# Two-layer hybrid decoder trunk: mixer with projections by halves, an earlier values product, regrouped output pairs, and modulation rows issued two ahead

## The chip, the cores and the metric

The kernel runs on one core of one Trainium2 chip. The metric is the device time of one execution in microseconds (us); the median of the runs is compared. The core's engines are TensorE (PE, matmuls; PEld for its weight loads), VectorE (DVE), ScalarE (ACT), GpSimd (POOL) and SyncE (SP), whose queue issues nearly all the DMAs here.

## The reference

Two layers over a sequence of 256 tokens of width 1024, in float32. Each layer is a half-step SwiGLU FFN, a token mixer and a second half-step FFN. Every sublayer has an RMS norm with a shift, a scale and a gate (nine modulation vectors of 1024 per layer), which come from a conditioning vector by a product with `w_ada`.

```
mod = split(silu(c) @ w_ada[l] + b_ada[l], 9)
h = rms_norm(x, ffn1_norm) * (1 + mod[1]) + mod[0]
x = x + 0.5 * (1 + mod[2]) * swiglu(h, ffn1_w_gu, ffn1_w_down)
h = rms_norm(x, mix_norm) * (1 + mod[4]) + mod[3]
x = x + (1 + mod[5]) * hybrid_mixer(h, ...)
h = rms_norm(x, ffn2_norm) * (1 + mod[7]) + mod[6]
x = x + 0.5 * (1 + mod[8]) * swiglu(h, ffn2_w_gu, ffn2_w_down)
```

The mixer projects h to a query latent (384), a key/value latent (256), a rotary key (32) and three convolution parts (512 each). The latents are normalised and expanded to 8 heads, followed by causal attention. The convolution group is a gate times a causal convolution of three taps. Both groups are normalised, concatenated and projected back to 1024. One RMS norm ends the trunk.

## The kernel before, in words

**Data.** Channels lie on the 128 partitions, tokens on the free axis: `x` is 8 tiles of 128 x 256. A float32 product is made of reduced-precision float32 matmuls: a factor is split into a high part (ScalarE, a copy into `fp32r`) and a low part (VectorE, the difference), and `mm3` sums high x high, high x low and low x high, three matmuls of 256 columns per 128 x 128 tile of weights. `mm3w` does the same with one matmul of 512 columns and one of 256.

**The weight stream.** All weights are a stream of chunks of 16 tiles (128 x 2048, 1 MB), numbered in the order of use: 22 gate/up and 11 down chunks for an FFN, 17 for a mixer. `load` (L235) takes the next one: a DMA on SP into `raw`, then high pieces on ScalarE (L262) and low pieces on VectorE (L265), two pieces for a chunk in the FFNs, four for most in the mixer. `raw`, `hi` and `lo` have three buffers each. Chunks 0 to 32 are layer 0's first FFN, 33 to 49 its mixer.

**The modulation rows.** The products with `w_ada` are 144 row tiles of 128 x 1024 (0.5 MB), each read by a DMA on SP (`ada_load`, L180) into one of four buffers and reduced by one VectorE instruction (L189) to a column of `mods`. `PACE` says how many rows must be done by which chunk (`ada_target`): in the down projection of layer 0's first FFN about two a chunk and more, in the mixers 6 over 16 chunks, in layer 0's second FFN and layer 1's first about one a chunk. In `load`, the chunk's DMA comes first and then its rows: DMA and product.

**Who sets the order.** SP runs its instructions in program order everywhere. TensorE does so in the mixer. A planner at compile time orders the others: it walks through a modelled time and gives each engine, among the instructions that are ready, the one that is due first. `due` sets the due time relative to a clock of matmul work; the `SLACK` table, `SPLIT_LEAD` and `ADA_SLACK` are such offsets. An instruction due late is still run early if its engine has nothing else ready. The order on each engine is then fixed, and the chip follows it, waiting where something is late.

**The mixer.** `ORDER` (L42) is the order of its steps, a letter each:
- `K`, `Q`, `P`: the projections to the key/value latent, the query latent, and its last third with the rotary key; four steps of 12 matmuls each make the two outputs of a chunk (`proj`, L604). `c` and `d` are the convolution's input and its gates, four chunks' and two chunks' worth of steps.
- `X`: the sum over channels for the mixer's RMS norm (a float32 matmul with a tile of ones, `Stat.rstd`). `L`, `Z`: the same for the latents. `N`, `V`, `v`: keys and values.
- `q0` to `q3`, `s0` to `s3`, `t0` to `t3`, `a0` to `a3`: queries, scores and softmax, transposes, and the product with the values of a head pair. `av_part` (L736) also copies the product out and adds its square to the attention's statistic.
- `n`, `m`: the sum and the norm of the attention output and of the convolution output.
- `A`, `B`: the output projection's steps over the two halves (`out`, L779). After every second `B` step a pair of output channels tiles is whole: residual (L394), then `put` for each tile, which makes the next FFN's input `u` in two parts (L351, L357) and adds the tile's square to the next norm's statistic (L318, L322).
- `w`: loads the next chunk ahead of its use. After `m`, a guard makes all later splits and modulation products follow the last instructions of m's norm.

`residual` and `put` also end the down projection of an FFN, so that the mixer's first step stands behind them.

Of the kernel before, what the change touches and what calls it, by code (L numbers as in the profile page):

```python
# [18 lines left out]
P = 128  # L19
L = 2  # L20
D = 1024
S = 256
KD = D // P
FF = 2816
NJ = FF // P
# [6 lines left out]
CH = 16 * P  # L32
WHOLE = 4
ADA_SLACK = 10000
ROPE_SLACK = 20000
LATE = 4
PACE = (0, 0), (8, 16), (21, 32), (33, 58), (49, 64), (84, 97), (117, 130), (133, 136), (146, 144)
# [1 line left out]
ENGS = {'p': mybir.EngineType.PE, 's': mybir.EngineType.SP, 'v': mybir.EngineType.DVE, 'a': mybir.EngineType.Activation}  # L39
MAN = 'sp'  # L40
SM_ACT = 2
ORDER = ("K K K X K Q Q P Q Q P P L c c c P c N Z V v q0 q1 s0 q2 c c c c t0 s1 a0 q3 c c c t1 c a1 s2 s3 c c c c t2 d d a2 t3 d d a3 "  # L42
         "d n w d w d d A A A w m A A w A A A B B B B B B B B").split()
WIN = dict(K=0, Q=1, P=2, c=3, d=7)
WO = dict(A=0, B=2)
SLACK = {'B': 6000, 'K': -2000, 'L': -4000, 'N': 0, 'P': 6000, 'Q': 0, 'V': 1000, 'X': 6000, 'Z': -4000, 'a': -4000, 'c': 6000, 'd': 0, 'm': 6000, 'n': 0, 'q': 2000, 's': -6000, 't': -4000}
CUTS = 4
GUARD = ('m',)
MIX_SPLIT, MIX_ADA = 2000, 2000
# [5 lines left out]
ADA_ORDER = [(0, m * 8 + i) for i in range(8) for m in (1, 0)]  # L55
# [64 lines left out]
def trunk(ctx: ExitStack, tc, x_d, c_d, pos_d, small_d, cst_d, ada_d, gu1_d, dn1_d, win_d, up_d, wo_d, gu2_d, dn2_d, out_d):  # L120
# [25 lines left out]
    x = one.tile([P, KD, S], F32, name="x")  # L146
# [4 lines left out]
    uL, uH = u[:, :, 0:S], u[:, :, S:]  # L151
# [59 lines left out]
    for l in range(L):  # L211
# [4 lines left out]
        n = {}  # L216
# [18 lines left out]
    def load(apart=False, head=False):  # L235


        i = taken[0]
        taken[0] += 1
        src, n, cuts = stream[i][:3]  # L240
        z0 = stream[i][3] if len(stream[i]) > 3 else 0
        raw = wp.tile([P, CH], F32, tag="raw", name=nm("raw"), bufs=3)
        hi = wp.tile([P, CH], F32R, tag="hi", name=nm("hi"), bufs=3)
        lo = wp.tile([P, CH], F32R, tag="lo", name=nm("lo"), bufs=3)
        if head:
            ada_load(1)
            nc.sync.dma_start(raw[:, :z0], src[:, :z0])
            ada_load(2)
            nc.sync.dma_start(raw[:, z0:n], src[:, z0:n])
        else:  # L250
            due(-LOAD_LEAD)
            nc.sync.dma_start(raw[:, :n], src)
            due(lead[1])
            with ExitStack() as es:
                for q in guard:
                    es.enter_context(tc.issue_after(q))
                ada(ada_target(i + 1))
        c = (n - z0) // cuts
        zs = [slice(z0 + q * c, z0 + (q + 1) * c) for q in range(cuts)]

        def top(q):
            nc.scalar.activation(hi[:, zs[q]], raw[:, zs[q]], AF.Copy)  # L262

        def rest(q):
            nc.vector.tensor_tensor(lo[:, zs[q]], raw[:, zs[q]], f32(hi[:, zs[q]]), ALU.subtract)  # L265

        if apart:
            return (raw, hi, lo), top, rest
        with ExitStack() as es:
            for q in guard:  # L270
                es.enter_context(tc.issue_after(q))
            for q in range(cuts):
                due(c / 128 * 322 * q - lead[0])
                top(q)
                rest(q)
        return raw, hi, lo
# [4 lines left out]
    def due(t):  # L281

        tc.cur_priority = int(clock[0] + t)
# [6 lines left out]
    def mm3(dst, w, t, aH, aL, first, last, ext=0):  # L290
        hi, lo = w[-2:]
        n = S + ext
        wh = hi[:, t * P:(t + 1) * P]
        wl = lo[:, t * P:(t + 1) * P]
        mm(dst[:, :n], wh, aH[:, :n], start=first, stop=False, skip_group_check=True)
        mm(dst[:, :S], wh, aL, start=False, stop=False, skip_group_check=True)
        mm(dst[:, :n], wl, aH[:, :n], start=False, stop=last, skip_group_check=True)
# [61 lines left out]
    class Pre:  # L359
# [20 lines left out]
            nc.scalar.activation(hcol, sh, AF.Copy)  # L380
            nc.vector.tensor_tensor(lcol, sh, f32(hcol), ALU.subtract)

        def put(self, k):
            g = self.scale(k)
            hi_of(uH[:, k, :S], x[:, k, :], g)
            lo_of(uL[:, k, :], uH[:, k, :S], x[:, k, :], g)
            self.stat.add(x[:, k, :])


    def residual(src, m, l, sub, f, halves=False):  # L390
# [177 lines left out]
    def mixer(l, pre, nxt):  # L568
        mf = one.tile([P, NJ, S], F32, tag="aH", name=nm("mf"))
        mr = one.tile([P, NJ, S], F32R, tag="aL", name=nm("mr"))  # L570
        ckv, cq, conv, V, K = mf[:, 0:2], mf[:, 2:5], mf[:, 5:9], mf[:, 9:13], mf[:, 13:21]
# [32 lines left out]
        def proj(t, evac):  # L604

            n = seen[t] = seen.get(t, -1) + 1
            if n % 4 == 0:
                open_[t] = chunk(), ps_tile()
            w, pt = open_[t]
            i = n % 4 // 2  # L610
            for k in range(n % 2 * 4, n % 2 * 4 + 4):
                mm3(pt[:, i, :], w, i * KD + k, uH[:, k, :], uL[:, k, :], k == 0, k == KD - 1, 2)
            if n % 4 == 3:
                due(SLACK[t])
                evac(scaled(pt))
# [163 lines left out]
        def out(t):  # L779
            n = seen[t] = seen.get(t, -1) + 1  # L780
            half = "AB".index(t)
            zH, zL = ((atH, atL), (cvH, cvL))[half]
            g, i = divmod(n, 4)
            if not acc:
                acc.extend((ps_tile(), ps_tile()))
            if i == 0:
                open_[t] = chunk()
            w = open_[t]
            steps = [(m, i) for m in range(4)] if half == 0 else [(m, k) for k in range(i % 2 * 2, i % 2 * 2 + 2) for m in
                                                                  (i // 2 * 2, i // 2 * 2 + 1)]  # L790
            for m, k in steps:
                m += 4 * g
                dst = acc[m // 2 % 2][:, g, (m % 2) * S:(m % 2 + 1) * S]
                mm3(dst, w, m % 4 * 4 + k, zH[:, k, :], zL[:, k, :], half == 0 and k == 0 and m % 2 == 0, half == 1 and k == 3)
            if half == 1 and i % 2 == 1:
                due(SLACK["B"])
                for q in (i - 1, i):
                    m = 4 * g + q
                    residual(acc[m // 2 % 2][:, g, (m % 2) * S:(m % 2 + 1) * S], m, l, 1, 1.0)
                    nxt.put(m)  # L800
                    if m == 5:
                        nxt.shifts()

        do = dict(K=lambda: proj("K", kv_evac), Q=lambda: proj("Q", q_evac), P=lambda: proj("P", qk_evac),
                  c=lambda: proj("c", conv_evac), d=lambda: proj("d", gate_evac), X=lambda: pre.stat.rstd(r, t=SLACK["X"]), L=kv_norm, N=keys, Z=q_norm,
                  V=lambda: values(0), v=lambda: values(1), n=lambda: head_norm("n", sat, attn, O_AN, atH, atL),
                  m=lambda: head_norm("m", scv, conv, O_CN, cvH, cvL), A=lambda: out("A"), B=lambda: out("B"))
# [96 lines left out]
def _layout(a):  # L904
    g = {}
# [17 lines left out]
    for f in (1, 2):  # L923
        t = _tiles(a[f"ffn{f}_w_gu"]).reshape(L, KD, 2, NJ, P, P)
        w = t.transpose(0, 3, 4, 1, 2, 5).reshape(L, NJ, P, CH)
        if f == 1:
            head = w[0, :8].reshape(8, P, 8, 2, P).transpose(2, 1, 0, 3, 4).reshape(1, 8, P, CH)
            w = np.concatenate([np.concatenate([head, w[:1, 8:]], axis=1), w[1:]], axis=0)
        g[f"gu{f}"] = np.ascontiguousarray(w)
        t = _tiles(a[f"ffn{f}_w_down"]).transpose(0, 2, 1, 3, 4).reshape(L, 11, 16, P, P)  # L930
# [6 lines left out]
    for i, s in [(i, s) for i in range(4) for s in (1, 2)] + [(i, 0) for i in range(4)]:  # L937
        parts.append(w[:, :, o + s * CW + i * P:o + s * CW + (i + 1) * P])
    t = _tiles(np.concatenate(parts, axis=2))
    t = t.transpose(0, 2, 1, 3, 4).reshape(L, 9, 16, P, P)  # L940
    g["win"] = np.ascontiguousarray(t.transpose(0, 1, 3, 2, 4).reshape(L, 9, P, CH))
    uk = a["w_ukv"].reshape(L, 2, P, H, 128)
    nope = uk[..., :64].reshape(L, 2, P, 4, P).transpose(0, 2, 3, 1, 4).reshape(L, P, 1024)
# [30 lines left out]
```

## Time and profile before

| what | value |
| --- | --- |
| median of 3 runs | 999.11 us (997.51 to 999.49) |
| the profiled execution | 1002.27 us |
| its span, first to last instruction | 1000.5 us |
| mean granted clock of TensorE | 0.994 |
| DMA moved | 250.78 MB, mean 251 GB/s |

All rows are of the profiled execution. A timeline row gives the start in us from the start of the span, the duration, the engine, the line of the kernel, the operation, out<-in by the program's names, the form, the count of instructions merged, and in brackets the engine's idle time before it with what ended it. SPq is SP's queue of DMAs: its rows are the issues, and a wait of the queue shows as a late issue. A row of waits gives total us, times, and the longest.

### The profile page before, as it was taken

Reading aid. Unit: us, or ns where it says so; the run is one execution under the profiler, and the core shown is the slowest. Engines: PE = TensorE matmul, PEld = TensorE weight load, DVE = VectorE, ACT = ScalarE, POOL = GpSimd, SP = SyncE. Lnnn points to the kernel's source line nnn. Section 1 sums busy time; section 2 is a strip of 40 time slices with the busy share of each in tenths; the row PEclk is TensorE's granted clock in tenths of the full one; section 3 lists DMA queues with packets and bytes.
Section 4 is the critical chain, followed back from the end, with each engine's and each line's share of the span. In section 5 each row is a group of like instructions: output and inputs, shape, how many; then the busy total and the mean of one; then the engine's idle time right before and its main releaser. Section 6 shows DMA issues by size and latency. Waiting matters only on the chain.

```text
span 1000.5 us, 16812 instructions
## 1 busy us (share of the span) xinstructions
PE 977.1 (98%) x6560; PEld 898.1 (90%) x6560; DVE 854.1 (85%) x1598; ACT 581.3 (58%) x1010; POOL 8.0 (1%) x27
## 2 busy tenths in 40 slices
PE   9999999999999999999999999998999999999996
PEld 7999998899989988888998888888998998888885
DVE  5899999999999998988899878877799999766653
ACT  4465544467856755654486555543687676656541
POOL 0000110000000000000000000000000000000000
PEclk9999999999999999999999999998999999999998
DMA  9999998874746687877768777776355547655531
GB/s 348 376 361 340 336 320 324 311 282 154 275 178 253 234 318 253 301 267 291 270 219 324 279 258 283 277 255 214 124 217 193 200 171 290 215 178 201 173 122 43
DMA packets 47007, 250.78 MB, mean 251 GB/s; under 512 B 5504, under 2 KB 5824, under 8 KB 26576
## 3 DMA queue, kind: packets, MB, share of 16 engines
q1 hardware_dynamic: 46224, 248.81, 68.3%
q8 instruction: 51, 0.84, 0.3%
q10 hardware_dynamic: 288, 0.65, 0.2%
q0 software_dynamic: 416, 0.25, 0.1%
q14 instruction: 28, 0.23, 0.1%
HBM read 248.59 MB, written 1.10 MB: 250 GB/s over the span
## 4 chain that ended last, share of the span: by engine, by line
PE 78%; DVE 11%; DMA 7%; issue 1%; ACT 1%; SPq 0%; DVEq 0%; ACTq 0%
PE ps L287 78%; DMA ada<-in_ada 6%; DVE lo L265 5%; DVE ada L189 1%; DVE x L394 1%; DMA raw<-in_gu 1%; DVE acc L322 1%; DVE u L357 1%; PE ps L731 1%; DVE mr L355 1%; ACT hi L262 0%; DMA cb<-in_c 0%; DVE nt L594 0%; ACT mr L351 0%; DVE mf L767 0%
## 5 line engine op out<-in xcount | busy, mean ns | idle before, releaser
L287 PE MATMUL ps<-u,hi 128*128 128x256 f32 (+2 forms) x2464 | 599.8, 324 | 6.5 <-ACT u L351 3.7
L287 PE MATMUL ps<-u,lo 128*128 128x256 f32 (+1 forms) x1664 | 470.1, 283 | 1.1 <-DVE lo L265 1.1
L287 PEld LDWEIGHTS ps<-u,hi 128*128 128x128 f32 x2464 | 413.5, 190 | 46.4 <-ACT u L351 4.3
L265 DVE TENSOR_TENSOR lo<-raw,hi 128x1024 fp32r<-128x1024 f32 (+2 forms) x384 | 394.8, 1046 | 41.4 <-ACT hi L262 40.9
L262 ACT ACTIVATE hi<-raw 128x1024 fp32r<-128x1024 f32 (+2 forms) x384 | 338.3, 912 | 113.4 <-PE ps L287 48.9
L287 PEld LDWEIGHTS ps<-u,lo 128*128 128x128 f32 x1664 | 315.9, 190 | 1.4 <-DVE lo L265 1.4
L287 PE MATMUL ps<-a,hi 128*128 128x512 f32 (+1 forms) x792 | 248.6, 372 | 1.4 <-DVE a L355 1.4
L189 DVE CUSTOM_DVE_ANT_0 ada<-ada,cb,small 128x1024 f32<-128x1024 f32 x144 | 183.1, 1280 | 33.4 <-DMA ada<-in_ada 32.8
L287 PE MATMUL ps<-a,lo 128*128 128x256 f32 x704 | 197.9, 281 | 0.0
L287 PEld LDWEIGHTS ps<-a,hi 128*128 128x128 f32 x792 | 143.0, 189 | 29.8 <-DVE a L355 1.7
L287 PEld LDWEIGHTS ps<-a,lo 128*128 128x128 f32 x704 | 133.2, 189 | 0.0
L351 ACT ACTIVATE a<-cc 128x256 fp32r<-128x256 f32 x88 | 36.3, 415 | 68.0 <-DVE cc L413 56.3
L287 PE MATMUL ps<-mr,hi 128*128 128x256 f32 x384 | 70.6, 285 | 0.0
L351 ACT ACTIVATE u<-x,gs 128x256 fp32r<-128x256 f32 x40 | 20.3, 507 | 84.6 <-DVE x L394 84.6
L287 PEld LDWEIGHTS ps<-mr,hi 128*128 128x128 f32 x384 | 60.2, 192 | 0.8 <-issue 0.3
L287 PE MATMUL ps<-mr,lo 128*128 128x256 f32 x192 | 54.3, 283 | 0.0
L394 DVE SCALAR_TENSOR_TENSOR x<-ps,gate,x 128x256 f32<-128x256 f32 x76 | 35.9, 480 | 19.2 <-PE ps L287 18.5
L355 DVE TENSOR_TENSOR a<-cc,a 128x256 fp32r<-128x256 f32 x88 | 37.0, 422 | 16.0 <-ACT a L351 15.8
L412 ACT ACTIVATE cc<-g 128x256 f32<-128x256 f32 x54 | 22.5, 418 | 41.5 <-DVE g L411 41.5
L411 DVE TENSOR_TENSOR g<-ps,g 128x512 f32<-128x512 f32 x54 | 37.0, 685 | 0.7 <-ACT g L410 0.6
L287 PEld LDWEIGHTS ps<-mr,lo 128*128 128x128 f32 x192 | 36.8, 191 | 0.0
L410 ACT ACTIVATE g<-ps 128x512 f32<-128x512 f32 x54 | 31.2, 578 | 0.0
(121 smaller groups left out, 568.4 us busy)
## 6 DMA issues: line engine op xcount, KB each, us to landing
raw<-in_gu SPq DMA_DIRECT2D x87, 1024.0 KB, 5.8
ada<-in_ada SPq DMA_DIRECT2D x144, 512.0 KB, 6.2
raw<-in_dn SPq DMA_DIRECT2D x44, 1024.0 KB, 5.2
raw<-in_win SPq DMA_DIRECT2D x18, 1024.0 KB, 5.7
raw<-in_wo SPq DMA_DIRECT2D x8, 1024.0 KB, 4.8
raw<-in_up SPq DMA_DIRECT2D x2, 1024.0 KB, 5.9
raw<-in_up SPq DMA_DIRECT2D x2, 768.0 KB, 4.4
raw<-in_up SPq DMA_DIRECT2D x4, 384.0 KB, 3.1
```

The lines of the kernel that those rows point to most:

```text
L189: nc.vector.tensor_tensor_reduce(out=a, in0=a, in1=cb, scale=1.0, scalar=sm(l, t), op0=ALU.mult, op1=ALU.add, accum_out=mods[l][:, t:t + 1])
L262: nc.scalar.activation(hi[:, zs[q]], raw[:, zs[q]], AF.Copy)
L265: nc.vector.tensor_tensor(lo[:, zs[q]], raw[:, zs[q]], f32(hi[:, zs[q]]), ALU.subtract)
L287: nc.tensor.matmul(dst, a, b, **kw)
L322: nc.vector.tensor_tensor(self.acc, self.acc, t, ALU.add)
L351: nc.scalar.activation(dH, src, AF.Copy, scale=scale)
L355: nc.vector.tensor_tensor(dL, src, f32(dH), ALU.subtract)
L357: nc.vector.scalar_tensor_tensor(dL, src, scale, f32(dH), ALU.mult, ALU.subtract)
L394: nc.vector.scalar_tensor_tensor(x[:, m, :], s, g, x[:, m, :], ALU.mult, ALU.add)
L410: nc.scalar.activation(t2, pg[:, :, :S], AF.Copy)
L411: nc.vector.tensor_tensor(t2, pg[:, :, S:], t2, ALU.add)
L412: nc.scalar.activation(sg, t2[:, 0, :], AF.Silu)
```

## The change

Five edits:
1. `proj` runs its four steps as two halves of the input channels: steps 0 and 1 take channels 0-3 of the first and the second output, steps 2 and 3 take channels 4-7. The host lays the tiles of the projection chunks out in that order. At the mixer's start `K K K X K Q Q P Q Q P P` becomes `K K Q Q K X K Q Q P P P`.
2. `t3 d d a3 d n` becomes `t3 d a3 d d n`: a3 one `d` step earlier, n where it was.
3. One `w` less, the others later: the chunks of A are asked for one by one, the first of B after `m`, the second at its use.
4. After a pair of output tiles, both residuals come first, then both `put` without the square, and then both squares with a due time of their own (`y`). The pair's due time falls from 6000 to 1500 ns, and to 0 for the last pair.
5. From chunk 33 on (`AHEAD_FROM`), `load` issues the rows' DMAs before the chunk's, and up to two rows beyond the target. The products stay with their chunk.

```
+ADA_AHEAD, AHEAD_FROM = 2, NJ + 11
...
-ORDER = ("K K K X K Q Q P Q Q P P L c c c P c N Z V v q0 q1 s0 q2 c c c c t0 s1 a0 q3 c c c t1 c a1 s2 s3 c c c c t2 d d a2 t3 d d a3 "
-         "d n w d w d d A A A w m A A w A A A B B B B B B B B").split()
+ORDER = ("K K Q Q K X K Q Q P P P L c c c P c N Z V v q0 q1 s0 q2 c c c c t0 s1 a0 q3 c c c t1 c a1 s2 s3 c c c c t2 d d a2 t3 d a3 "
+         "d d n d w d d A A A w m A A w A A A B B B B B B B B").split()
...
-SLACK = {'B': 6000, 'K': -2000, ...
+SLACK = {'B': 1500, 'y': 5000, 'K': -2000, ...
...
             due(-LOAD_LEAD)
+            if i >= AHEAD_FROM:
+                ada_load(min(ada_target(i + 1) + ADA_AHEAD, len(ADA_ORDER)))
             nc.sync.dma_start(raw[:, :n], src)
...
-        def put(self, k):
+        def put(self, k, add=True):
...
-            self.stat.add(x[:, k, :])
+            if add:
+                self.stat.add(x[:, k, :])
...
-            i = n % 4 // 2
-            for k in range(n % 2 * 4, n % 2 * 4 + 4):
-                mm3(pt[:, i, :], w, i * KD + k, uH[:, k, :], uL[:, k, :], k == 0, k == KD - 1, 2)
+            i, h = n % 2, n % 4 // 2
+            for k in range(4 * h, 4 * h + 4):
+                mm3(pt[:, i, :], w, 4 * (n % 4) + k % 4, uH[:, k, :], uL[:, k, :], k == 0, k == KD - 1, 2)
...
-                due(SLACK["B"])
-                for q in (i - 1, i):
-                    m = 4 * g + q
+                pair = 4 * g + i - 1, 4 * g + i
+                due(SLACK["B"] if n < 7 else 0)
+                for m in pair:
                     residual(acc[m // 2 % 2][:, g, (m % 2) * S:(m % 2 + 1) * S], m, l, 1, 1.0)
-                    nxt.put(m)
-                    if m == 5:
-                        nxt.shifts()
+                for m in pair:
+                    nxt.put(m, False)
+                if n == 5:
+                    nxt.shifts()
+                due(SLACK["y"])
+                for m in pair:
+                    nxt.stat.add(x[:, m, :])
...
-    t = t.transpose(0, 2, 1, 3, 4).reshape(L, 9, 16, P, P)
+    t = t.transpose(0, 2, 1, 3, 4).reshape(L, 9, 2, 2, 4, P, P).swapaxes(2, 3).reshape(L, 9, 16, P, P)
```

More of the change, by code (lines that the diff above doesn't have):

```diff
@@ L41 @@
 SM_ACT = 2
-ORDER = ("K K K X K Q Q P Q Q P P L c c c P c N Z V v q0 q1 s0 q2 c c c c t0 s1 a0 q3 c c c t1 c a1 s2 s3 c c c c t2 d d a2 t3 d d a3 "
-         "d n w d w d d A A A w m A A w A A A B B B B B B B B").split()
+ORDER = ("K K Q Q K X K Q Q P P P L c c c P c N Z V v q0 q1 s0 q2 c c c c t0 s1 a0 q3 c c c t1 c a1 s2 s3 c c c c t2 d d a2 t3 d a3 "
+         "d d n d w d d A A A w m A A w A A A B B B B B B B B").split()
 WIN = dict(K=0, Q=1, P=2, c=3, d=7)
 WO = dict(A=0, B=2)
-SLACK = {'B': 6000, 'K': -2000, 'L': -4000, 'N': 0, 'P': 6000, 'Q': 0, 'V': 1000, 'X': 6000, 'Z': -4000, 'a': -4000, 'c': 6000, 'd': 0, 'm': 6000, 'n': 0, 'q': 2000, 's': -6000, 't': -4000}
+SLACK = {'B': 1500, 'y': 5000, 'K': -2000, 'L': -4000, 'N': 0, 'P': 6000, 'Q': 0, 'V': 1000, 'X': 6000, 'Z': -4000, 'a': -4000, 'c': 6000, 'd': 0, 'm': 6000, 'n': 0, 'q': 2000, 's': -6000, 't': -4000}
 CUTS = 4
```

## The prediction

> **What bounds the kernel now.** I read the page first, then TensorE's busy time in stretches of 10 us, then its own rows wherever a stretch was not full, and from each of those back to what released it.
>
> ```profile
> PE 977.1 (98%) x6560; PEld 898.1 (90%) x6560; DVE 854.1 (85%) x1598; ACT 581.3 (58%) x1010; POOL 8.0 (1%) x27
> ```
>
> TensorE (PE) is busy for 977.1 of 1000.5 us. In a full stretch it starts a 256-column matmul every 0.12 us, and nothing in the change takes a matmul away. So the change can only move TensorE's waits. These are the waits next to the code it touches, from TensorE's timeline (start, duration, then the idle time before it and what ended it):
>
> ```profile
> 206.99 0.39 PE L287 MATMUL ps<-u,lo 128*128 128x258 f32 x1 [1.14 <-DVE lo L265]
> ...
> 283.29 0.67 PE L287 MATMUL ps<-acc,ones 128*128 128x256 f32 x2 [1.47 <-DVE acc L322]
> ...
> 317.15 0.38 PE L287 MATMUL ps<-u,hi 128*128 128x258 f32 x1 [0.41 <-ACT u L351]
> ...
> 318.53 0.38 PE L287 MATMUL ps<-u,hi 128*128 128x256 f32 x1 [1.00 <-DVE u L357]
> ...
> 694.73 0.39 PE L287 MATMUL ps<-u,hi 128*128 128x258 f32 x1 [2.59 <-ACT u L351]
> ...
> 695.78 0.58 PE L287 MATMUL ps<-u,hi 128*128 128x256 f32 x1 [0.67 <-DVE u L357]
> ...
> 772.41 0.67 PE L287 MATMUL ps<-acc,ones 128*128 128x256 f32 x2 [1.47 <-DVE acc L322]
> ...
> 806.44 0.38 PE L287 MATMUL ps<-u,hi 128*128 128x258 f32 x1 [0.69 <-ACT u L351]
> 807.82 0.38 PE L287 MATMUL ps<-u,hi 128*128 128x256 f32 x1 [1.00 <-DVE u L357]
> ```
>
> Each layer has three places: the mixer's first projection (206.99; 694.73 and 695.78), the sum "n" over the attention output (283.29; 772.41), and the way out into the second FFN (317.15 and 318.53; 806.44 and 807.82). Together the waits are 10.4 us. The wait at 694.73 costs more than itself, as stretches of TensorE show (us, busy time and count of each engine, then granted clock, DMA share, GB/s):
>
> ```profile
> 210.00:220.00 10.00, 10.00 (x85) 9.95 (x84) 9.42 (x19) 6.55 (x15) 0.00 (x0) 1.00 0.92 333
> 695.05:701.90 6.85, 6.18 (x27) 5.94 (x27) 3.49 (x9) 1.81 (x4) 0.00 (x0) 0.50 0.37 115
> ```
>
> After it the clock is 0.50 for 6.85 us. There 27 matmuls take 6.18 us; at 85 in 10 us they take 3.2, and some 0.3 more for the two float32 ones of the statistic: about 2.7 us lost.
>
> **The change part by part: projection by halves.** K and Q now do their channels 0-3 first (K K Q Q), so channels 4-7 are asked for after 48 matmuls, 48 x 0.12 = 5.7 us, not after 12, 1.4 us. Layer 1's wait is for channel 7:
>
> ```profile
> 689.46 0.41 PE L287 MATMUL ps<-u,hi 128*128 128x258 f32 x2
> ...
> 687.81 1.89 DVE L265 TENSOR_TENSOR lo<-raw,hi 128x512 fp32r<-128x512 f32 x3
> ...
> 685.29 1.01 SPq L180 DMA_DIRECT2D ada<-in_ada  x1
> ...
> 692.44 1.28 DVE L189 CUSTOM_DVE_ANT_0 ada<-ada,cb,small 128x1024 f32<-128x1024 f32 x1 [2.74 <-DMA ada<-in_ada]
> 693.65 0.48 DVE L394 SCALAR_TENSOR_TENSOR x<-ps,gate,x 128x256 f32<-128x256 f32 x1
> ...
> 695.25 0.48 DVE L357 SCALAR_TENSOR_TENSOR u<-x,gs,u 128x256 fp32r<-128x256 f32 x1
> ```
>
> VectorE (DVE) stands 2.74 us before a modulation product whose row has not landed, and the residual of channel 7 is queued behind it. Even if this repeats, the channel is whole at 695.73. The projection starts at 689.46, and by halves it asks for channel 7 after 57 matmuls, near 696.3. So both waits go, 2.59 + 0.67, and the slow clock with them: **-6.0 us**. Bounds: nothing gained if Q's weights, now asked for 2.9 us after the start, are late instead; -6.0 if not. I take -6.0, as Q's last low piece is done at 689.70 (687.81 + 1.89). The statistic X stands at 60 matmuls, 7.2 us in, and hides as well. K's evacuation has two steps less before the key norm L; its cover falls from 10 to 7.2 us, and I take nothing, bound +1.
>
> **Rows issued further ahead.** From the mixer of layer 0 on, SP issues rows up to two beyond the target, and ahead of the weight chunk. Each row's DMA waits for a slot of four, that is for the product of the row four before, and the chunk is queued behind it on SP. Where one row goes with each chunk, the product four back is long done, so this costs nothing (if not, a chunk still has its three buffers of cover). Nor does it save much there. VectorE waits for rows 28 times, because products are placed as soon as the planner thinks that a row has landed, whichever row it is, and TensorE is covered in nearly all of these:
>
> ```profile
> DVE ada L189 <- DMA ada<-in_ada: 32.8, 28, 3.2
> ```
>
> But at the first chunk of layer 0's mixer two extra rows come at once, right after a stretch with two rows and more a chunk:
>
> ```profile
> 195.07 1.28 DVE L189 CUSTOM_DVE_ANT_0 ada<-ada,cb,small 128x1024 f32<-128x1024 f32 x1
> ...
> 196.28 1.28 DVE L189 CUSTOM_DVE_ANT_0 ada<-ada,cb,small 128x1024 f32<-128x1024 f32 x1
> ...
> 201.56 1.28 DVE L189 CUSTOM_DVE_ANT_0 ada<-ada,cb,small 128x1024 f32<-128x1024 f32 x1
> ```
>
> ```profile
> 196.40 0.33 SPq L180 DMA_DIRECT2D ada<-in_ada  x1
> 196.82 0.38 SPq L252 DMA_DIRECT2D raw<-in_win  x1
> ...
> 202.32 1.15 ACT L262 ACTIVATE hi<-raw 128x512 fp32r<-128x512 f32 x2 [2.83 <-DMA raw<-in_win]
> ...
> 205.44 0.40 PE L287 MATMUL ps<-u,hi 128*128 128x258 f32 x2
> ...
> 206.24 1.29 DVE L265 TENSOR_TENSOR lo<-raw,hi 128x512 fp32r<-128x512 f32 x2
> ```
>
> The last row before K's chunk goes out at 196.40, when the product of 195.07 has ended (196.35). The next two rows then need the products of 196.28 and of 201.56; the latter ends at 202.84. K's chunk follows 0.42 later, at 203.3, not 196.82. Its first split can start 5.5 us after issue, as now (202.32 - 196.82): 208.8; a high piece takes 1.15 / 2, so TensorE starts at 209.4; the low piece (1.29 / 2) makes its third matmul 210.1, not 206.99: **+3.1 us**. TensorE, which has nothing left from 205.5, then stands for 3.9 us, longer than the 2.59 that halved the clock, so I add the same **+2.7**. Bounds: -1.1 (the present wait goes) where the slot is free sooner, +5.8 where all of this holds. I take +5.8: the products before 201.56 are tied to work that the change doesn't touch.
>
> [...]
>
> **Values product further ahead of the sum.** The last product a3 moves one d-step (12 matmuls, 1.44 us) forward, and n keeps its place:
>
> ```profile
> 276.27 0.48 PE L287 MATMUL ps<-u,hi 128*128 128x258 f32 x2
> ...
> 276.76 0.80 ACT L734 ACTIVATE pT<-ps 128x768 f32<-128x768 f32 x1
> ...
> 280.36 0.36 ACT L747 ACTIVATE mf<-ps 128x256 f32<-128x256 f32 x1
> 280.63 1.14 ACT L262 ACTIVATE hi<-raw 128x512 fp32r<-128x512 f32 x2
> 281.67 0.40 ACT L318 ACTIVATE acc<-mf 128x256 f32<-128x256 f32 x1
> 281.98 0.71 ACT L318 ACTIVATE sq<-mf 128x256 f32<-128x256 f32 x2
> ```
>
> n is late by 1.47 because the square of a3's output comes after weight splits on ScalarE (ACT). Starting 1.44 earlier leaves next to nothing of it. What a3 reads, pT, is ready at 277.56 and is asked for one step after t3, 276.27 + 1.44 = 277.7: just in time, at most 0.2 lost. What moves with it are two matmul groups, a copy, a square and an addition; no DMA. I take -1.3 a layer, **-2.6**; bounds 0 (the planner fills the gap with splits again) and -2.9.
>
> **Output pairs.** Residuals and u come ahead of splits, and square sums 5 us later. But there is one w less, so the load of the output's first B chunk now comes after m, and the guard holds its splits behind m's norm. The order of the DMAs on SP stays: a w only says from when on a chunk's splits are due. This is what VectorE does in that stretch:
>
> ```profile
> 299.00:318.50 19.50, 18.11 (x147) 17.50 (x146) 19.50 (x40) 13.37 (x26) 0.00 (x0) 1.00 0.66 251
> 787.60:808.10 20.50, 18.82 (x154) 18.30 (x153) 20.50 (x43) 14.03 (x28) 0.00 (x0) 1.00 0.60 223
> ```
>
> ```profile
> 290.76 0.69 DVE L265 TENSOR_TENSOR lo<-raw,hi 128x512 fp32r<-128x512 f32 x1
> ...
> 298.93 1.28 DVE L189 CUSTOM_DVE_ANT_0 ada<-ada,cb,small 128x1024 f32<-128x1024 f32 x1
> 300.14 0.08 DVE L189 DVE_READ_ACCUMULATOR2_ANT mod<- 128x1 f32 x1
> 300.14 4.77 DVE L265 TENSOR_TENSOR lo<-raw,hi 128x512 fp32r<-128x512 f32 x6
> ```
>
> VectorE is full from 299 to 318.5: it is the bound there, and four low pieces (4 x 1.29 / 2 = 2.6 us), which begin at 290.76 now, come on top. Against that, what must precede u of channel 7 gets less: square sums and the second FFN's later splits go behind it. So the waits of 1.41 and 1.69 shrink, though not to nothing. I take -1.0 a layer, **-2.0**; bounds -3.1 (all of it) and +5.2 (the pieces in full, 2.6 a layer).
>
> **The sum**: -6.0 + 3.1 + 2.7 - 2.6 - 2.0 = **-4.8 us**. The profiled execution has a span of 1000.5 and took 1002.27; this makes it 995.7 and 997.5. The median of the runs shown is 999.11, 3.2 below the profiled one, so I set it at **994.3**.
>
> **The rivals.**
> - *Layer 0's chunk is not late* (the product of 201.56 moves ahead). Then -1.1 stands for +5.8: -11.7, 987.4. For it: the product's row may have landed long before. Against: VectorE's order up to there has no new work in it.
> - *Layer 0's wait doesn't halve the clock*: -7.5, 991.6. For it: waits of 1.14 to 1.47 don't. Against: 2.59 does, and 3.9 is longer.
> - *The slow clock of layer 1 is the profiled run's alone*: the runs lie 3.2 below it. Then -6.0 is -3.3: -2.1, 997.0.
> - *Slower: VectorE pays for the moved splits.* The four low pieces lengthen the way out by 2.6 us a layer, to waits near 4 us; from 2.59 in one piece on they halve the clock, 2.7 more. Twice 5.3 in place of -2.0 makes +7.8: 1006.9. For it: no free VectorE time in either stretch. Against: the new order lets splits wait before u does.
>
> **How the numbers follow.** Forecast 0.44 (its own range 990.5 to 998), late chunk absent 0.16, no slow clock in layer 0 0.13, slow clock only under the profiler 0.12, slower 0.15. This kernel's measurement can tell 0.2%, 2 us: faster is below 997.1, slower above 1001.1. Faster: 0.36 of the forecast, all of the next two, 0.05 of the fourth, 0.70. Same: 0.08 + 0.07 = 0.15. Slower: 0.15. The range 987 to 1001 leaves out part of the first rival and the slower one, 0.2 in all.
>
> **What would show it.** In the profile after: the first mixer matmul of layer 1 with no wait and a clock of 1.00; in layer 0 two row DMAs right ahead of K's chunk, the second issued when a product ends, the chunk some 6 us later than now, TensorE idle near 3.9 us and a clock of 0.50 behind it; n's waits under 0.3; the B chunk's splits behind m's norm, and the waits at the way out about half. I am wrong if layer 0's chunk goes out before 200, or if the way out gets longer.

## The result and the profile after

The changed kernel is **slower**, by 0.6%: 1004.56 us, median of 12 runs (1001.29 to 1009.57), against 999.95 for 12 runs of the kernel before beside it; ratio 1.0059, 95% interval [1.0036, 1.0081]. All ratios below compare fast runs alone, which leaves out two of the ten runs of the kernel with a3 alone (1932.95 and 5439.51 us). The forecast was 994.3, with 987 to 1001 as its range. The profiled execution after has a span of 1006.2 us against 1000.5, +5.7 where -4.8 was forecast.

TensorE's row of busy time, kernel after:

```profile
PE 981.1 (98%) x6560; PEld 902.1 (90%) x6560; DVE 852.1 (85%) x1598; ACT 583.1 (58%) x1010; POOL 8.1 (1%) x27
```

The count of matmuls is the same, and PE's busy time is 4.0 us longer, at a mean granted clock of 0.989 against 0.994: the clock is 0.50 for 17.0 us in three pieces (from 208.25, 334.55 and 648.58 us), before for 6.8 in one, the end of each span aside. Where TensorE waits, its timeline shows (kernel after, its rows with a wait at the places of the prediction, in the second FFNs and in layer 1's first FFN; the row of 292.68 comes again in layer 1, at 784.04):

```profile
210.38 0.80 PE L290 MATMUL ps<-u,hi 128*128 128x258 f32 x2 [4.12 <-ACT hi L265]
...
292.68 0.84 PE L290 MATMUL ps<-mr,hi 128*128 128x256 f32 x2 [0.26 <-ACT mr L354]
...
324.18 0.70 PE L290 MATMUL ps<-acc,ones 128*128 128x256 f32 x2 [0.95 <-DVE acc L325]
...
333.98 0.51 PE L290 MATMUL ps<-u,hi 128*128 128x258 f32 x2 [3.39 <-ACT hi L265]
336.95 0.58 PE L290 MATMUL ps<-u,lo 128*128 128x258 f32 x1 [2.46 <-DVE lo L268]
...
647.53 0.51 PE L290 MATMUL ps<-a,hi 128*128 128x512 f32 x1 [1.89 <-DVE a L358]
...
814.82 0.48 PE L290 MATMUL ps<-acc,ones 128*128 128x256 f32 x1 [0.42 <-DVE acc L325]
```

Line numbers of after are one to four higher than before (L290 is the matmul, L265 and L268 the splits, L190 the modulation product, L181 and L255 the DMAs of rows and chunks). The waits forecast to go have gone: nothing is left at layer 1's mixer start (704.08), at the sums n (287.50 and 778.86) and at u on the way out. Small new ones stand behind them: 0.26 us at the first `A` step of each layer, 0.95 and 0.42 us at the sum of the second FFN's norm. The wait forecast to come has come (4.12 at 210.38), and by the way that was forecast. SP, kernel after:

```profile
197.06 6.80 SPq L181 DMA_DIRECT2D ada<-in_ada  x3
203.96 0.86 SPq L255 DMA_DIRECT2D raw<-in_win  x2
```

The third of these rows goes out when the product of 202.22 has ended (203.50), and K's chunk behind it, at 203.96 where before it was 196.82. At 330 to 337 us, in layer 0's second FFN, stand waits that the prediction does not have.

Cut at TensorE's first matmul of each stage, the two profiled executions compare so (us; the column "forecast" sorts the prediction's terms into the same stages):

| stage | before | after | difference | forecast |
| --- | --- | --- | --- | --- |
| up to layer 0's mixer, and the mixer | 312.02 | 317.16 | +5.1 | +4.5 |
| layer 0's second gate/up | 126.64 | 134.15 | **+7.5** | -1.0 |
| layer 0's second down | 62.32 | 62.32 | 0.0 | 0 |
| layer 1's first FFN | 188.48 | 190.45 | +2.0 | 0 |
| layer 1's mixer | 111.85 | 104.43 | -7.4 | -7.3 |
| layer 1's second gate/up | 126.64 | 125.10 | -1.5 | -1.0 |
| the rest | 72.6 | 72.6 | 0.0 | 0 |

One stage holds most of the miss. Its stretch in each kernel, the one before first (us, busy time and count of PE, PEld, DVE, ACT and POOL, then the granted clock, DMA share, GB/s):

```profile
312.02:438.66 126.64, 125.22 (x772) 112.28 (x771) 118.62 (x202) 80.51 (x132) 0.00 (x0) 1.00 0.75 271
```

```profile
335.00:340.00 5.00, 3.05 (x14) 3.05 (x15) 5.00 (x10) 4.52 (x8) 0.00 (x0) 0.50 1.04 400
317.16:451.31 134.15, 127.35 (x773) 114.27 (x771) 125.89 (x216) 80.40 (x130) 0.00 (x0) 0.97 0.75 283
```

The waits of 0.95, 3.39 and 2.46 us stand where before there were 1.41; that is 5.4 us. The other 2.1 are longer busy time (127.35 against 125.22 us), with the clock of 0.50 behind the waits. What TensorE waits for at 333.98 and 336.95 is the third gate/up chunk, number 52. Its way, kernel after: SP's queue, VectorE's products (with the low piece at 335.68) and ScalarE's high piece.

```profile
304.91 0.33 SPq L181 DMA_DIRECT2D ada<-in_ada  x1
307.32 0.33 SPq L255 DMA_DIRECT2D raw<-in_gu  x1
325.42 0.33 SPq L181 DMA_DIRECT2D ada<-in_ada  x1
325.86 0.37 SPq L255 DMA_DIRECT2D raw<-in_gu  x1
```

```profile
303.60 1.28 DVE L190 CUSTOM_DVE_ANT_0 ada<-ada,cb,small 128x1024 f32<-128x1024 f32 x1
...
324.11 1.28 DVE L190 CUSTOM_DVE_ANT_0 ada<-ada,cb,small 128x1024 f32<-128x1024 f32 x1
...
332.89 1.04 ACT L265 ACTIVATE hi<-raw 128x1024 fp32r<-128x1024 f32 x1
...
335.68 1.22 DVE L268 TENSOR_TENSOR lo<-raw,hi 128x1024 fp32r<-128x1024 f32 x1
```

Followed back from the chunk: its DMA goes out at 325.86; ahead of it on SP stands row 68 (325.42), which needs the slot of row 64, that is product 64, at 324.11 to 325.39. The product before it, 63, runs at 303.60, right behind the last step of m's norm: it is held there by the guard, since its chunk is now loaded after m. Product 64 then finds VectorE full, 18.44 of 19.23 us, with work that the planner puts first:

```profile
304.88:324.11 19.23, 18.35 (x148) 17.64 (x146) 18.44 (x43) 12.62 (x26) 0.00 (x0) 1.00 0.24 83
```

In the kernel before the same chunk goes out at 302.66:

```profile
302.66 0.33 SPq L252 DMA_DIRECT2D raw<-in_gu  x1
```

So the chunk goes out 23.2 us later. Of these, 5.1 are the later start of the whole stage: before, the chunk goes out 9.4 us ahead of the stage's start, after 8.7 us behind it. The other 18.1 us are more than its three buffers cover. SP's waits for products grew accordingly, from 75.4 us in all (the longest 6.7) to 128.2 (the longest 17.8).

Layer 1 has the same delay: a row goes out at 821.61, chunk 137 behind it at 822.03, where it went at 802.79 before (12.0 us later, counted from the start of its stage). But 137 is the fifth chunk of its FFN and not the third, and TensorE shows no wait for it.

### The profile page after: what moved, and what is told of

It reads as the page before. It is cut to its first block, busy times and chain, and to the rows that moved or that the text cites. A ratio compares the mean times of both kernels' runs of the same rounds, so it can differ in the third digit from the quotient of the medians.

```text
span 1006.2 us, 16836 instructions
## 1 busy us (share of the span) xinstructions
PE 981.1 (98%) x6560; PEld 902.1 (90%) x6560; DVE 852.1 (85%) x1598; ACT 583.1 (58%) x1010; POOL 8.1 (1%) x27
## 4 chain that ended last, share of the span: by engine, by line
PE 73%; DVE 15%; DMA 8%; issue 2%; ACT 1%; SPq 0%; DVEq 0%; ACTq 0%
PE ps L290 72%; DMA ada<-in_ada 6%; DVE lo L268 6%; DVE ada L190 3%; DVE g L415 1%; DVE acc L325 1%; DMA raw<-in_win 1%; DVE x L398 1%; PE ps L735 1%; DVE nt L528 1%; DMA raw<-in_gu 1%; DVE u L360 1%; PE ps L446 1%; ACT hi L265 0%; DMA x<-in_x 0%
## 5 line engine op out<-in xcount | busy, mean ns | idle before, releaser
L290 PE MATMUL ps<-u,hi 128*128 128x256 f32 (+2 forms) x2464 | 599.5, 324 | 7.5 <-ACT hi L265 7.5
L290 PE MATMUL ps<-u,lo 128*128 128x256 f32 (+1 forms) x1664 | 471.0, 283 | 2.5 <-DVE lo L268 2.5
L290 PEld LDWEIGHTS ps<-u,hi 128*128 128x128 f32 x2464 | 414.5, 191 | 46.1 <-ACT hi L265 7.9
L268 DVE TENSOR_TENSOR lo<-raw,hi 128x1024 fp32r<-128x1024 f32 (+2 forms) x384 | 394.4, 1046 | 40.2 <-ACT hi L265 39.7
L265 ACT ACTIVATE hi<-raw 128x1024 fp32r<-128x1024 f32 (+2 forms) x384 | 336.8, 912 | 95.7 <-issue 40.8
L290 PEld LDWEIGHTS ps<-u,lo 128*128 128x128 f32 x1664 | 316.6, 190 | 2.9 <-DVE lo L268 2.9
L290 PE MATMUL ps<-a,hi 128*128 128x512 f32 (+1 forms) x792 | 250.1, 373 | 1.9 <-DVE a L358 1.9
L190 DVE CUSTOM_DVE_ANT_0 ada<-ada,cb,small 128x1024 f32<-128x1024 f32 x144 | 182.9, 1280 | 28.3 <-DMA ada<-in_ada 28.1
L290 PE MATMUL ps<-a,lo 128*128 128x256 f32 x704 | 198.6, 282 | 0.0
L290 PEld LDWEIGHTS ps<-a,hi 128*128 128x128 f32 x792 | 143.8, 190 | 30.5 <-DVE a L358 2.2
L290 PEld LDWEIGHTS ps<-a,lo 128*128 128x128 f32 x704 | 133.9, 190 | 0.0
L290 PE MATMUL ps<-mr,hi 128*128 128x256 f32 x384 | 71.3, 286 | 0.7 <-ACT mr L354 0.5
L290 PEld LDWEIGHTS ps<-mr,hi 128*128 128x128 f32 x384 | 60.3, 191 | 2.2 <-ACT mr L354 0.9
L290 PE MATMUL ps<-mr,lo 128*128 128x256 f32 x192 | 54.7, 285 | 0.0
L290 PEld LDWEIGHTS ps<-mr,lo 128*128 128x128 f32 x192 | 36.7, 191 | 0.8 <-DVE lo L268 0.8
```

What stands on the lines that cost most here:

```text
L190: nc.vector.tensor_tensor_reduce(out=a, in0=a, in1=cb, scale=1.0, scalar=sm(l, t), op0=ALU.mult, op1=ALU.add, accum_out=mods[l][:, t:t + 1])
L290: nc.tensor.matmul(dst, a, b, **kw)
```

## The experiments

Theory R: the loss is the rows that stand ahead of two chunks on SP. Rival V, the prediction's slower rival: VectorE pays for the B chunk's splits that the missing `w` put behind m. Short names: the "four w" order is `d d n w d w d d A A A w m` in place of `d d n d w d d A A A w m`.

**1. The change without rows ahead.**

```
-ADA_AHEAD, AHEAD_FROM = 2, NJ + 11
+ADA_AHEAD, AHEAD_FROM = 2, 1000
```

> The changed kernel without edit 5 (no modulation row ahead of a chunk, none beyond the target); edits 1 to 4 stay, so the first B chunk's splits still come behind m's norm. Theory R (the rows queued ahead on SP make two chunks of layer 0 late): TensorE starts layer 0's mixer with the old wait of about 1.1 us (clock 1.00), and the waits of 0.95, 3.39 and 2.46 us at 324 to 337 us with the half clock behind them are gone. In the profile the stage up to the mixer gets 4.9 shorter and layer 0's second gate/up stage 7.5, so about 12 us less than the changed kernel, near 993 us, 0.7% below the kernel before. Rival V (VectorE pays for the splits that the missing w put behind m): only the first part goes, the second gate/up stage stays 7.5 longer than before, and the time is near 999 to 1000 us, the same as before.

Measured: 993.74 us, ratio to before 0.9962 [0.9943, 0.998]. TensorE's first wait in layer 0's mixer, its longest in the second gate/up stage and one in layer 1's first FFN, then the stretch of that stage, this kernel:

```profile
206.92 0.39 PE L290 MATMUL ps<-u,lo 128*128 128x258 f32 x1 [1.14 <-DVE lo L268]
...
336.82 0.47 PE L290 MATMUL ps<-u,hi 128*128 128x512 f32 x1 [1.10 <-DVE u L358]
...
507.14 0.39 PE L290 MATMUL ps<-u,hi 128*128 128x258 f32 x1 [1.91 <-ACT u L354]
```

```profile
311.49:437.95 126.46, 124.92 (x773) 112.21 (x772) 118.84 (x202) 78.36 (x128) 0.00 (x0) 1.00 0.77 278
```

The old 1.14 is back at the start, and the gate/up stage takes 126.46 us and not 134.15, with the splits still behind m. Both parts of the loss hang on edit 5, and V in its full form falls. The gain is 0.4% where 0.7% was expected: this execution has waits for VectorE that the expectation did not have (1.10 at 336.82, 1.91 and 0.81 at 507 to 508, 1.55 at 636.89).

**2. The products let out of the guard.** Splits stay behind m's norm, rows stay ahead.

```
-                for q in guard:
-                    es.enter_context(tc.issue_after(q))
-                ada(ada_target(i + 1))
+            ada(ada_target(i + 1))
```

> The changed kernel, but the modulation products of a chunk asked for after m are not held behind m's norm; only the weight splits are. Rows ahead and the later w stay. In VectorE's order product 63 moves from instruction 527 to 422 and product 64 from 563 to 477, ahead of m's norm (which ends at 532 instead of 526, two products later). Theory R: rows 67 and 68 find their slots free, the third gate/up chunk of layer 0's second FFN (chunk 52) goes out some 20 us earlier, near 303 us, and the 7.5 us of that stage are gone: near 997 us; layer 0's late first mixer chunk stays. Two products (2.6 us) ahead of m's norm may cost up to that much at the step after m. Rival V: the splits are where they were, so the stage stays 7.5 us longer than before: near 1004 us.

Measured: 996.16 us, 0.9989 [0.9968, 1.0009]. SP's queue, then TensorE's waits and the stretch of the stage, this kernel:

```profile
309.35 0.33 SPq L255 DMA_DIRECT2D raw<-in_gu  x1
```

```profile
209.29 0.50 PE L287 MATMUL ps<-u,hi 128*128 128x258 f32 x2 [4.06 <-ACT hi L262]
...
292.45 0.84 PE L287 MATMUL ps<-mr,hi 128*128 128x256 f32 x2 [1.34 <-ACT mr L351]
298.08 0.70 PE L287 MATMUL ps<-acc,ones 128*128 128x256 f32 x2 [0.71 <-DVE acc L322]
```

```profile
317.32:442.37 125.05, 124.72 (x772) 112.09 (x771) 118.43 (x201) 79.72 (x132) 0.00 (x0) 1.00 0.75 282
```

Chunk 52 goes out at 309.35, and the stage takes 125.05 us: the 7.5 us are gone though the splits still come behind m's norm, so it was the held product that made the chunk late. The two products now stand ahead of m's norm (290.26 and 296.39 on VectorE), and TensorE waits 1.8 us more there: 1.34 where 0.26 stood, and 0.71 at the sum m where there was none. The mixer's start is as late as in the change (4.06).

**3. The fourth w back, rows ahead kept.**

```
-         "d d n d w d d A A A w m A A w ...
+         "d d n w d w d d A A A w m A A w ...
```

> The changed kernel with the fourth w back: 'd d n w d w d d' in place of 'd d n d w d d', so the first B chunk is asked for before m and neither its splits nor its product (63) are held behind m's norm; rows ahead stay. In VectorE's order product 63 moves from instruction 527 to 422, product 64 from 563 to 532. Theory R: row 67 goes out before m, row 68 behind product 64, which comes right behind m's norm near 299 us; so chunk 52 goes out near 301 us instead of 325.9, the 7.5 us of that stage are gone, and the time is near 997 us. Rival V says the same of this kernel; the pair of this run and the one with free products tells them apart.

Measured: 995.41 us, 0.9982 [0.9967, 0.9998]. SP's queue and TensorE's wait at that place, this kernel:

```profile
304.02 0.33 SPq L181 DMA_DIRECT2D ada<-in_ada  x1
306.43 0.33 SPq L255 DMA_DIRECT2D raw<-in_gu  x1
324.47 0.33 SPq L181 DMA_DIRECT2D ada<-in_ada  x1
324.89 1.32 SPq L255 DMA_DIRECT2D raw<-in_gu  x1
```

```profile
335.11 0.39 PE L290 MATMUL ps<-u,lo 128*128 128x258 f32 x1 [1.34 <-DVE lo L268]
```

Chunk 52 is in time (306.43). The stall has moved one chunk on: row 69 waits for product 65, chunk 53 goes out at 324.89, and TensorE waits 1.34 us for it. One product earlier in VectorE's order was worth one chunk on SP here.

**4. Rows ahead alone on the kernel before.**

```
+ADA_AHEAD, AHEAD_FROM = 2, NJ + 11
...
+            if i >= AHEAD_FROM:
+                ada_load(min(ada_target(i + 1) + ADA_AHEAD, len(ADA_ORDER)))
             nc.sync.dma_start(raw[:, :n], src)
```

> The kernel before with edit 5 alone: rows two ahead, and ahead of the chunk, from chunk 33 on. Four w as before. Theory R: layer 0's first mixer chunk is late, TensorE waits near 4 us and runs at half clock behind it: +5 us up to the mixer; product 64 stands at instruction 529, right behind m's norm, so chunk 52 is not late and the second gate/up stage of layer 0 costs nothing more; layer 1 keeps its wait of 2.59 us and half clock unless the rows bring its last products of the first FFN's down projection earlier. Near 1005 us (+5). A rival in which a burst of rows only uses slots that are free says no change: 1000 us.

Measured: 1000.97 us, 1.0027 [1.0006, 1.0049]. The wait at the mixer's start is there, with no other edit:

```profile
209.79 0.51 PE L290 MATMUL ps<-u,hi 128*128 128x258 f32 x2 [4.25 <-ACT hi L265]
```

Layer 0's second gate/up stage took 126.68 us, as before (126.64). The sum is +2.7 us and not +5. Layer 1's mixer started without its wait in this profile, but run 12 below shows that this wait comes and goes in the kernel before itself, so what makes the difference stays open.

**5. Rows ahead only from chunk 72 on, four w** (edits 1, 2, 4 whole).

```
-ADA_AHEAD, AHEAD_FROM = 2, NJ + 11
+ADA_AHEAD, AHEAD_FROM = 2, 72
...
-         "d d n d w d d A A A w m A A w ...
+         "d d n w d w d d A A A w m A A w ...
```

> The changed kernel with the fourth w back (as in the run with the fourth w) and the rows ahead only from chunk 72 on, the down projection of layer 0's second FFN; so SP's order is the old one at layer 0's first mixer chunk and at its second gate/up stage, and the new one in layer 1. Theory R: layer 0 has the old wait of 1.1 us at the mixer's start in place of 4.1 us and a half clock, its second gate/up stage takes 125 to 126.5 us, and layer 1's first FFN and mixer take what they take with the fourth w (124.5, 62.0, 104.1 us). From the span of 994.0 without rows ahead, less the 3.2 us at 505 us and the 2.2 us at 635 us that rows ahead save: a span near 988.5 and a time of about 988, 1.0% below the kernel before. Rival: the waits at 505 and 635 us in the run without rows are chance of the order and come back here: 994, 0.4% below.

Measured: 987.77 us, 0.9906 [0.9872, 0.994], span 986.0: what theory R gave.

**6 to 8. The other edits one by one** on the kernel before: halves, a3, output pairs. Halves is edit 1's hunks, pairs is edit 4's with its `SLACK`, both as in the diff above; a3 is one step of `ORDER` (four w stay):

```
-... t2 d d a2 t3 d d a3 d n w d w d d A A A w m ...
+... t2 d d a2 t3 d a3 d d n w d w d d A A A w m ...
```

> The kernel before with edit 1 alone (K and Q by halves and the order K K Q Q K X K Q Q P P P). The prediction's term: both waits at layer 1's mixer start (2.59 and 0.67 us) go and the half clock of 6.85 us with them: -6.0 us, near 992. In layer 0 the wait of 1.1 us for K's low piece stays. Rival: the slow clock is the profiled run's alone, so -3.3 us, near 995; or Q's weights are late in place of channel 7, and nothing is gained.

> The kernel before with edit 2 alone (a3 one d-step earlier). The prediction's term: n's wait of 1.47 us falls to some 0.2 us in each layer: -2.6 us, near 995.7; the way out is as before (1.41 and 1.69 us). Rival: the planner fills the gap with weight splits on ScalarE again, n waits as long as before, and the time is the same.

> The kernel before with edit 4 alone (the pairs' residuals and u ahead of the squares, due times 1500, 0 and 5000 ns); four w and the old row order. The prediction's term: the waits at the way out (1.41 us in layer 0, 1.69 in layer 1) shrink by 1.0 us each: -2.0 us, near 996.3. Rival: VectorE is full there and what is put later only moves the wait to the second FFN's first chunks: the same time.

| edit alone | ratio | in us of 998.6 | forecast |
| --- | --- | --- | --- |
| halves | 0.9974 [0.9954, 0.9994] | -2.6 (-4.6 to -0.6) | -6.0 |
| a3 earlier | 0.9953 [0.9922, 0.9984] | -4.7 (-7.8 to -1.6) | -2.6 |
| output pairs | 0.9928 [0.9898, 0.9958] | -7.2 (-10.2 to -4.2) | -2.0 |

With halves alone, layer 1's mixer starts without a wait. With a3 alone, the wait of 1.47 us at n is gone in both layers, and 0.26 us stand at the first `A` step. With the pairs alone, the waits at the way out are gone in both layers and the second gate/up stages run without a gap (pairs alone, layer 0 and layer 1):

```profile
311.59:436.04 124.45, 124.45 (x773) 112.12 (x772) 118.32 (x201) 79.87 (x131) 0.00 (x0) 1.00 0.76 276
791.88:916.33 124.45, 124.45 (x772) 112.12 (x771) 100.28 (x161) 79.89 (x130) 0.00 (x0) 1.00 0.60 213
```

That is 126.64 - 124.45 = 2.2 us a layer. The three single values add up to -14.5 us, while the kernels with all three edits (runs 9 and 15) measure -7.3 and -8.2. So the single values cannot be added up. In a3's profile, for one, layer 1's mixer starts without its wait, which a3 does not touch. The rest of the difference stays open.

**9 and 10. Edits 1, 2 and 4 together, four w, no row ahead; and the same without the halves.**

```
-ADA_AHEAD, AHEAD_FROM = 2, 72
+ADA_AHEAD, AHEAD_FROM = 2, 1000
```

(against the fifth run; the tenth also takes edit 1's hunks away)

> Edits 1, 2 and 4 on the kernel before, four w, no row ahead anywhere: the kernel of the run with rows from chunk 72 on, less those rows. If rows ahead earn something in layer 1 (there VectorE stood 2.63 us before a row that had not landed and TensorE then 1.91 and 0.81 us at 505 us, and 1.55 us at 635 us, in the run without rows), these waits come back here: +4 us on 987.8, near 992. If those waits belonged to the missing w or to chance: 988.

> Edits 2 and 4 on the kernel before: the run of three edits less the projection by halves. If halves are worth what the prediction said, layer 1's mixer start waits again for channel 7: 1.1 to 2.6 us and 0.67 us, with a half clock where the wait is long: +2 to +6 us on the run of three edits. If the other edits alone bring channel 7 in time: no difference.

Measured: 990.85 us, 0.9927 [0.9902, 0.9953], and 994.74 us, 0.9959 [0.9933, 0.9984]. The medians are 3.9 us apart, which the halves would be worth, but the intervals overlap. Nor do the profiles show the 3.9 at the place that the prediction named: without the halves, layer 1's mixer starts with 0.67 us of wait, and 4.92 us stand at the turn from gate/up to down before it (0.61 in the ninth run).

**11. The chunk ahead of its rows on SP.**

```
             nc.sync.dma_start(raw[:, :n], src)
+            if i >= AHEAD_FROM:
+                ada_load(min(ada_target(i + 1) + ADA_AHEAD, len(ADA_ORDER)))
```

(and the same two lines taken away ahead of the chunk's DMA)

> The changed kernel with the order on SP turned round in load: the chunk's DMA first, then its rows, still up to two beyond the target; three w, and in VectorE's order product 63 stands at instruction 528 and 64 at 566 as in the changed kernel. Theory R (what is queued on SP behind a row that waits for its slot is late, whatever it is): layer 0's first chunk goes out at 196.8 and is not late; the next one (Q's) is behind row 59 until about 203.4 instead of 197.3, needed at 208.4 and whole near 209.5: some 1 us of wait, no half clock. In the second FFN, row 68, which needs product 64 (near 324 us), now stands behind chunk 52 and ahead of chunk 53: chunk 52 in time, chunk 53 issued near 325.9 and needed near 334.3, 2.8 us after it lands: a wait of 0 to 2 us in place of 6.8 and the half clock. Together 8 to 11 us off the changed kernel: near 995. If it were the number of rows in flight that costs (bandwidth), and not the place in the queue: no difference, near 1004.

Measured: 998.89 us, 0.9997 [0.9974, 1.0019]: 0.6% below the change's ratio, where 0.8 to 1.1% was expected. The stall went one chunk on at both places, as the queue says (SP at both, then TensorE):

```profile
197.25 0.38 SPq L253 DMA_DIRECT2D raw<-in_win  x1
198.03 5.60 SPq L181 DMA_DIRECT2D ada<-in_ada  x2
203.72 0.86 SPq L253 DMA_DIRECT2D raw<-in_win  x2
...
324.33 0.33 SPq L181 DMA_DIRECT2D ada<-in_ada  x1
324.76 1.60 SPq L253 DMA_DIRECT2D raw<-in_gu  x1
```

```profile
212.97 0.39 PE L290 MATMUL ps<-u,lo 128*128 128x258 f32 x1 [2.42 <-DVE lo L268]
...
334.90 0.39 PE L290 MATMUL ps<-u,lo 128*128 128x258 f32 x1 [1.60 <-DVE lo L268]
```

The same rows are in flight, so it is the place in the queue that costs. At the mixer TensorE waits 2.42 us for the second chunk and not 1: its high pieces start at 209.28, but two modulation products (209.82 to 212.31) stand ahead of its low pieces on VectorE.

**12 and 13. Both kernels once more,** unedited, for second profiles.

> The kernel before once more, for a second profile of the same program. If the half clock of 6.85 us at layer 1's mixer start belongs to the wait of 2.59 us, it is there again. [...]

> The changed kernel once more, for a second profile of the same program. If the two late chunks of layer 0 follow from the order of the instructions, TensorE waits 4.1 us at the mixer's start (near 206 us) and some 3.4 and 2.5 us near 330 to 337 us again, each within 0.5 us, with the half clock behind each for 3.4 or 6.9 us; the waits in layer 1's first FFN (1.89 us at 647 us) may differ by some us. If the stall at 330 us belonged to the profiled execution alone: it is gone, and the span is near 999.

The kernel before, again: span 1000.9 us, and no wait at all at layer 1's mixer start. Instead TensorE waits 5.42 us at the turn from gate/up to down in the FFN ahead of it, with the half clock there. The two rows below are of this second profile:

```profile
639.29 0.79 PE L287 MATMUL ps<-a,hi 128*128 128x512 f32 x1 [5.42 <-DVE a L355]
```

```profile
637.05:643.88 6.83, 4.59 (x14) 3.92 (x15) 5.67 (x9) 4.06 (x6) 0.00 (x0) 0.50 0.84 307
```

The kernel after, again: span 1001.7, and both places of layer 0 to a quarter of a microsecond:

```profile
210.21 0.55 PE L290 MATMUL ps<-u,hi 128*128 128x258 f32 x2 [4.35 <-ACT hi L265]
...
332.85 0.51 PE L290 MATMUL ps<-u,hi 128*128 128x258 f32 x2 [3.39 <-ACT hi L265]
335.82 0.58 PE L290 MATMUL ps<-u,lo 128*128 128x258 f32 x1 [2.46 <-DVE lo L268]
```

Its wait in layer 1's first FFN (1.89) is gone. So what the change does to layer 0 follows from the order of the instructions and is in both profiles; what stood between 630 and 700 us belongs to one execution. The spans of these second profiles differ by only 0.8 us, where the medians differ by 4.6: two single executions do not price a change.

**14 and 15. The fifth and the ninth kernel again, beside each other** (edits 1, 2 and 4 with and without rows from chunk 72 on).

> The kernel with edits 1, 2 and 4, four w, and rows ahead from chunk 72 on, once more, beside the same kernel without those rows on the same chip. If rows ahead earn something where VectorE waits for rows all through layer 1's first FFN: 2 to 4 us below the other, 987 to 988. If not, as the prediction said: the two agree within 1.5 us.

> The same kernel without rows ahead. If rows ahead earn something in layer 1: near 991, with 2 to 5 us of waits of TensorE for VectorE between 500 and 690 us. If not: as the run with rows from 72 on, within 1.5 us.

Measured: with rows 990.19 us, 0.9929 [0.9901, 0.9957]; without 987.91 us, 0.9918 [0.9888, 0.9949]. Rows ahead earn nothing that can be measured, even where they cost nothing. The waits at 507 and 637 us of the first experiment belonged to that execution or to its three w. The kernel with edits 1, 2 and 4, four w and no row ahead beats both kernels: 0.8% below the one before, about 1.4% below the change.

## Why the prediction was wrong

- **The step that failed**: "Where one row goes with each chunk, the product four back is long done, so this costs nothing (if not, a chunk still has its three buffers of cover)." In layer 0's second FFN the product four back ran at 324.11, the chunk went out 23.2 us later (18.1 counted from the start of the stage), and three buffers did not cover it: +7.5 us, or 8.5 more than the -1.0 forecast for that stage. The prediction had both halves in hand. It said that the missing `w` puts the B chunk's load after m and that the guard holds its splits; but it counted only the four low pieces, not the modulation product that the same `load` places. And it followed SP's queue at layer 0's mixer start, and nowhere else.
- **The slower rival** named the right place and the wrong cause. Not VectorE's time for the splits, but SP standing behind one product; the run with the products out of the guard has the same splits and no stall. A rest of V may be real: with three w and no rows ahead the stage takes 126.46 us, with four 124.44 (the row below, from run 9). But with three w and the products out of the guard it takes 125.05, so part of that rest too may be the held products.

```profile
311.16:435.60 124.44, 124.44 (x772) 112.11 (x771) 114.37 (x192) 77.14 (x126) 0.00 (x0) 1.00 0.73 264
```

- **Layer 0's mixer start, +5.8, was right** in mechanism and nearly in size: TensorE waited 4.12 us (3.9 forecast), and the clock halved (0.50 from 208.25 to 215.07). At 85 matmuls in 10 us, the pace at a clock of 1.00, the half clock costs 1.4 and 1.5 us where it lasts 3.41 us, in the second profile and in rows alone (16 matmuls in 3.23 and 3.39 us of busy time), and 2.3 in the first profile (20 in 4.68), where 6.82 us of it began inside the wait; 2.7 was put down. With the wait's growth from 1.14 to 4.12 us that makes 5.3. The +5.1 of the first stage is not this term alone: n's gain is taken off in it, and 0.8 us of it lie ahead of the mixer, where TensorE runs out of work at 206.26 and not at 205.44 (at 205.86 in the second profile).
- **Layer 1's mixer start, -6.0, was mis-sized.** The wait and its half clock were taken from one execution as a property of the kernel. The second profile has none there, and 5.42 us elsewhere. Halves alone measure -2.6 us. The rival that gave the slow clock to the profiled run alone (-3.3 for this term) is nearer.
- **n, -2.6: right.** Nothing is left of 1.47 us at n and of 0.2 at m in each layer, and 0.26 us are new at the first `A` step.
- **Output pairs, -2.0: too small.** The reason given, a VectorE that is full, is about load; the reorder works on what comes first. Alone it took the whole waits, the bound of -3.1 that was named and not chosen, with VectorE as full as before (19.50 of 19.50 us from 298.60 to 318.10). By the two stages' lengths it took 4.4 us.
- **Layer 1's first FFN, +2.0 in the profile, was not priced.** It is 0.5 us more wait and 1.5 us more busy time, with a clock of 0.50 behind the wait (648.58 to 651.98), and it is the part that varies between executions (1.39, 5.42, 1.89 and 0 us at the turn to down, two profiles of each kernel). What sets it off in a given execution stays open. VectorE stands before rows that have not landed in all of them, but rows ahead changed neither that (32.8 us before, 28.1 after) nor the time.

The stages add up to the +5.7 us of the two profiles: +5.1 + 7.5 + 2.0 - 7.4 - 1.5. That layer 1's mixer shows -7.4, close to its forecast, is luck in part: the first profile of the kernel before had the wait, its second had none.

## What to carry to other kernels

Here a row's DMA that waited for its buffer held the chunk behind it on SP's queue (chunk 52 went out 23.2 us later, and with the chunk ahead of its rows the stall went to the next chunk), so the prefetch moved ahead of a critical load cost what its slowest releaser cost: for each place where such a load is needed, look up when the instruction that frees the slot runs, not whether it usually has. When a load is moved behind a guard, list all that the same call issues, then ask which queue waits for each. And a wait that is to be priced should be seen in two executions: here the waits behind the late chunks came back within 0.3 us, and the one behind a row that had not landed (2.59 us) was gone the second time, with 5.42 us at another place.

## What was unexpected in the hardware

The half clock (0.50 in the rows) came in pieces of about 3.41 or 6.83 us. The kernel before has one of 6.83 (695.06); the kernel after has two of that length (208.25 and 334.55) and one of 3.41 (648.58), the piece that runs into the end of each span aside. This is the mixer's start of layer 0: after, after again and rows alone, after nearly the same wait (4.12, 4.35, 4.25 us):

```profile
208.25:215.07 6.82, 4.68 (x20) 4.46 (x21) 6.11 (x15) 4.51 (x9) 0.00 (x0) 0.50 1.01 423
```

```profile
210.54:213.95 3.41, 3.23 (x16) 3.02 (x15) 3.40 (x7) 3.10 (x7) 0.00 (x0) 0.50 1.02 425
```

```profile
210.50:213.91 3.41, 3.39 (x16) 3.39 (x17) 3.41 (x6) 2.99 (x6) 0.00 (x0) 0.50 1.02 425
```

In the first it begins inside the wait, in the others 0.3 to 0.7 us after its end. The length of the wait alone did not decide: with the halves alone, two waits of 0.41 and 1.00 us were followed by a piece of half clock (the first row below), while in the kernel before the same two waits were not (1.00 in its stretch 312.02:438.66), nor were 2.42 us with the chunk ahead of its rows (the second row).

```profile
319.38:322.79 3.41, 3.41 (x16) 3.23 (x16) 3.37 (x9) 1.99 (x4) 0.00 (x0) 0.50 0.86 324
```

```profile
210.55:217.38 6.83, 4.41 (x37) 4.38 (x37) 6.83 (x13) 3.12 (x6) 0.00 (x0) 1.00 0.86 320
```

So after such waits a piece followed in some executions and not in others, at some 1.5 us for each 3.41 us in which TensorE was busy (16 matmuls in 3.39 us in rows alone, 1.9 us at 85 in 10 us). With the nine waits of 3.39 us and more in the profiles of these runs (3.39 twice, 4.06, 4.12, 4.25, 4.27, 4.35, 4.92 and 5.42) it came each time, inside the wait or behind it. In 29 runs of the kernel before, those with a mean clock of 0.994 have a mean span of 999.1 us (7 runs), those with 0.997 one of 994.6 (5 runs): much of the spread between these runs goes with the clock.
